# Two attention and long-convolution layers on one core: the scheduler's durations for fp32r matmuls, 32-column products and dots changed, and six more 512-wide buffers

## The chip, the cores and the metric

The kernel runs as one program on one core of a Trainium2 chip. The metric is the device time of one execution in microseconds; the time of a kernel is the median over several executions. The engines are TensorE (PE in the profile, with its weight loads as PEld), VectorE (DVE), ScalarE (ACT), GpSimd (POOL) and SyncE (SP), which issues all DMAs of this kernel.

## The reference

Two layers work on 256 latent tokens (x) and 256 context tokens (ctx), 2048 wide, in fp32. Cut to what matters:

```python
def _layer(x, ctx, c, c_ctx, lp, cos, sin, update_ctx):
    sh_x, sc_x, g_x = _modulation(c, lp["ada_w"], lp["ada_b"])       # silu(c) @ ada_w + ada_b, split in 3
    sh_c, sc_c, g_c = _modulation(c_ctx, lp["ada_w"], lp["ada_b"])
    hx = rmsnorm(x, lp["pre_g"]) * (1.0 + sc_x) + sh_x
    hc = rmsnorm(ctx, lp["pre_g"]) * (1.0 + sc_c) + sh_c
    px = hx @ lp["w_in"]                                             # 2048 x 5952
    pc = hc @ lp["w_in"]                                             # in the last layer only the k/v columns
    ...                                                              # latent attention, 8 heads, on q/kv columns
    ...                                                              # Hyena: width-3 conv, implicit filters, FFT conv
    y = concatenate([rmsnorm(o_mla) * silu(p_gm), rmsnorm(y_h) * silu(p_gh)])
    x_new = x + g_x * rmsnorm(y @ lp["w_out"], lp["post_g"])         # ctx likewise, in the first layer
```

`_modulation` is a matrix product of two vectors (c and c_ctx) with a 2048 x 6144 matrix in each layer: little arithmetic, 50 MB of weights a layer.

## The kernel before

**Arithmetic.** Each fp32 product is made of three fp32r matmuls: a weight and a token tile are each split into a rounded part (hi, a cast on ACT) and the rest (lo, a subtraction on DVE), and `mm3` multiplies hi by hi, hi by lo and lo by hi. In the first layer context and latent tokens are one 512-wide moving operand; in the second, and in the first layer's output projection, it is 256 wide.

**The order is made by a scheduler in the kernel's own Python.** `Net.run` holds a clock for each engine, written by durations that the helpers give (`mm`, `act`, `tt`, `dot`, `dma`). Jobs are generators that yield one operation at a time. At each step the scheduler takes, of the operations that can start within `WINDOW` of the first, the one whose job has the lowest rank, emits it, and moves the clock. The instruction order on every engine thus hangs on those durations; on the chip each engine runs its queue in that order and waits on semaphores. The durations set no time on the chip.

**The main line of work** is a fixed list of items, one each for a 128x1024 tile of weights, handled by three jobs: `loader` (DMA into a buffer), `prepper` (the split) and `products` (the matmuls into the PSUM tiles `acc`). Beside it run the side jobs on PSUM tiles `mis`: filters (`filt`), attention (`pair_job`, `qk_job`, `head_job`), Hyena (`hy_job`), norms, and the boundary between the layers. Products have the last rank, so they fill PE where no side step is ready.

**Buffers.** SBUF holds five 1024-wide `raw` and two `hi` tiles, and 82 tiles `s` of 128x512 (`N_SLOTS`) that all jobs share. The loader takes a `raw` tile where one is free (one DMA of 512 KB), and otherwise two `s` tiles (two DMAs of 256 KB) if at least `SPARE_RAW` = 12 are spare; the prepper does likewise with `SPARE` = 8.

**The start.** The products of the first layer need the modulated input, and so the modulation weights. They come in two ways. Most blocks go through PE: `ada_first` (weights `in_p_ada_first`, 128x128 against the 32-column tile `cs`, "32-column products"). The rest go through DVE: `ada_slow` (weights `in_p_ada_slow`) loads a weight tile into a ring of three buffers (`N_RING`) and makes dot products with a row of c or c_ctx that is spread over the partitions (`s<-crow_d`), by `dot`, one or two for each tile. The next tile for a ring buffer can be loaded when the dots on the old one are done, and SP's queue is in order: what is queued behind that load waits too. The first wave that runs, 16 ring loads and 32 dots, makes the first layer's shift for the last four of the 16 blocks of model columns; it takes four rounds, each with its own two `crow_d` loads. The sections in `ada_rest` are 32-column products with 512 wide weights, spread over the first layer.

Lines of the profile: L232 is `mm`, L235 a transpose, L243 and L245 `act`, L250 the DVE helpers, L280 `dot`, L309 `dma`.

Of the kernel before, what the change touches and what calls it, by code (L numbers as in the profile page):

```python
# [19 lines left out]
KT = 16  # L20
# [10 lines left out]

N_RAW = 5
N_HI = 2
N_SLOTS = 96 - 2 * (N_RAW + N_HI)
RESERVE = 1
SPARE = 8
SPARE_RAW = 12
# [45 lines left out]
def free_size(ap):  # L83
    n = 1
    for s in ap.shape[1:]:
        n *= s
    return n
# [82 lines left out]
class Net:  # L170
    def __init__(self, tc, pools, a):
# [6 lines left out]
        self.owner = None  # L178
        self.slots = Slots(self, sb, "s", N_SLOTS, [P, 512])
        self.raws = Slots(self, sb, "raw", N_RAW, [P, 1024])  # L180
# [44 lines left out]
    def mm(self, out, lhsT, rhs, start=True, stop=True, share=1.0):  # L225
        n = free_size(rhs)
        if lhsT.dtype == F32R:
            c = max(n, 480 if n < 256 else 0) / 2400 + 0.0025
        else:
            c = 4 * (n / 2400 + 0.0025) * share if n > 1 else 0.11  # L230
        return Op("pe", c, [out], [lhsT, rhs],
                  lambda: self.nc.tensor.matmul(out, lhsT, rhs, start=start, stop=stop), 0.2)  # L232

# [42 lines left out]
        return op  # L276

    def dot(self, junk, a, b, acc):
        return Op("dve", 0.07 + free_size(a) * 0.00104, [junk, acc], [a, b],
                  lambda: self.nc.vector.scalar_tensor_tensor(out=junk, in0=a, scalar=1.0, in1=b, op0=ALU.mult,  # L280
                                                              op1=ALU.mult, accum_out=acc))

# [339 lines left out]
    def ada_rest(self, which, l, sec):  # L622
        hold = {}
        out = []
        for kt in range(KT):
            def load(raws, kt=kt):
                for h in range(2):
                    yield from self.load(raws[h], self.a["p_ada_rest"][which, kt, h])

            def pe(raws, kt=kt):  # L630
                if kt == 0:
                    (hold["ps"],) = yield from self.pget()
                ps = hold["ps"]
                for c in range(4):
                    yield self.mm(ps[32 * c:32 * c + 32, :], self.cs[:, kt, :],
                                  raws[c // 2][:, (c % 2) * 512:(c % 2) * 512 + 512],
                                  kt == 0, kt == KT - 1, share=0.27)

            def post(kt=kt):
                if kt == KT - 1:  # L640
                    self.job(f"ada{l}_{sec}", self.ada_cols(l, sec, hold["ps"], [(4 * b, 4 * b + 4) for b in range(4)]), want=1)
            out.append(Item(load, None, pe, post, nraw=2, halves=True))
        return out
# [1193 lines left out]
```

## Time and profile before

| | |
|---|---|
| median of 3 runs | 1464.53 us (1457.56 to 1468.52) |
| the profiled execution | 1457.93 us; its span 1456.2 us |
| PE, share of the span | 98% |
| PEld | 85% |
| DVE | 82% |
| ACT | 48% |
| DMA, mean rate | 226 GB/s |

The span runs from the first to the last instruction. PE's busy share is made of modelled ends: matmuls overlap in the pipeline, so a row with no idle time can still hold gaps of some tens of ns, and the pace is better read from how many matmuls stand in a stretch of the chain of waits.

### The profile page before, as it was taken

The numbers are of one execution on the slowest core, as the hardware profiler recorded it, in microseconds if no ns is written. First come the engines' busy times: TensorE is split into PE (matmuls) and PEld (weight loads), VectorE is DVE, ScalarE is ACT, GpSimd is POOL, SyncE is SP. The second block draws the span as 40 slices with busy tenths as digits, with TensorE's granted clock in tenths as the row PEclk, the third lists the DMA queues.
The fourth block names the chain that finished last, engine by engine and source line by source line (L and its number), as shares of the span: only waits on it lengthen the run. The fifth ranks groups of instructions, "written<-read, shape, count | busy, mean of one in ns | idle before, by whom it ended". The sixth has DMA issues, their size and how long they took to land.

```text
span 1456.2 us, 25519 instructions
## 1 busy us (share of the span) xinstructions
PE 1428.0 (98%) x9316; PEld 1240.0 (85%) x9316; DVE 1188.4 (82%) x2514; ACT 692.0 (48%) x1323; POOL 16.4 (1%) x20
## 2 busy tenths in 40 slices
PE   7899999999999999999999999999999999999997
PEld 5677787778788887777779999999999999999886
DVE  5578989897899888998888887888977888796554
ACT  5421354335354552344324444566655667655542
POOL 0000000000000000000000000000000000000000
PEclk9999999999999999999999999999999999999999
DMA  9998875568466776557968885467728334658541
GB/s 319 350 355 262 293 263 200 164 216 307 159 210 220 252 276 227 180 194 231 318 189 301 297 283 197 167 222 247 254 88 319 113 105 149 236 199 293 174 145 58
DMA packets 165870, 328.88 MB, mean 226 GB/s; under 512 B 18501, under 2 KB 41068, under 8 KB 165744
## 3 DMA queue, kind: packets, MB, share of 16 engines
q1 hardware_dynamic: 165744, 327.25, 65.8%
q8 instruction: 73, 1.20, 0.3%
q14 instruction: 53, 0.43, 0.1%
HBM read 301.99 MB, written 25.18 MB: 225 GB/s over the span
## 4 chain that ended last, share of the span: by engine, by line
PE 87%; DMA 8%; DVE 2%; issue 1%; SPq 1%; ACT 1%; DVEq 0%; POOLq 0%; POOL 0%; ACTq 0%
PE acc L232 68%; PE mis L232 17%; PE mis L235 3%; DMA s<-in_p_ada_first 2%; DMA raw<-in_p_ada_first 1%; DMA raw<-in_p_win 1%; DVE s L250 1%; DMA s<-in_p_win 1%; SPq L309 1%; DMA s<-in_ctx 1%; DMA s<-xt_d 1%; DVE junk L280 0%; DMA s<-in_p_uv 0%; DMA s<-crow_d 0%; DVE raw L250 0%
## 5 line engine op out<-in xcount | busy, mean ns | idle before, releaser
L232 PE MATMUL acc<-s,hi 128*128 128x256 f32 (+1 forms) x2304 | 563.0, 335 | 0.7 <-ACT hi L243 0.6
L232 PE MATMUL acc<-s,s 128*128 128x256 f32 (+1 forms) x2976 | 485.8, 318 | 0.0
L232 PEld LDWEIGHTS acc<-s,s 128*128 128x128 f32 x2976 | 425.8, 191 | 39.1 <-issue 2.7
L232 PEld LDWEIGHTS acc<-s,hi 128*128 128x128 f32 x2304 | 388.4, 190 | 53.0 <-issue 8.8
L250 DVE TENSOR_TENSOR s<-s,s 128x512 fp32r<-128x512 f32 (+5 forms) x575 | 342.2, 623 | 40.0 <-ACT s L245 19.3
L232 PE MATMUL acc<-s,raw 128*128 128x256 f32 (+1 forms) x1104 | 369.8, 335 | 0.1
L280 DVE SCALAR_TENSOR_TENSOR junk<-s,s 128x512 bf16<-128x512 f32 x352 | 241.5, 686 | 24.8 <-DMA s<-in_p_ada_slow 8.4
L232 PE MATMUL mis<-s,s 128*128 128x256 f32 (+1 forms) x1232 | 239.6, 337 | 0.9 <-ACT s L243 0.9
L232 PEld LDWEIGHTS acc<-s,raw 128*128 128x128 f32 x1104 | 210.0, 190 | 21.5 <-DVE raw L250 1.2
L232 PEld LDWEIGHTS mis<-s,s 128*128 128x128 f32 x1232 | 189.6, 189 | 30.0 <-ACT s L243 2.4
L243 ACT CAST s<-s 128x512 fp32r<-128x512 f32 (+3 forms) x324 | 180.6, 589 | 71.9 <-DVE s L250 28.5
L243 ACT CAST hi<-raw 128x1024 fp32r<-128x1024 f32 (+1 forms) x100 | 97.2, 972 | 123.4 <-PE acc L232 55.4
L250 DVE TENSOR_TENSOR raw<-raw,hi 128x1024 fp32r<-128x1024 f32 x88 | 107.3, 1220 | 20.7 <-ACT hi L243 19.9
L243 ACT CAST hi<-s 128x512 fp32r<-128x512 f32 x124 | 73.4, 618 | 96.6 <-PE acc L232 74.4
L250 DVE TENSOR_TENSOR raw<-s,hi 128x512 fp32r<-128x512 f32 x124 | 83.9, 687 | 36.8 <-ACT hi L243 35.9
L243 ACT COPY s<-mis 128x512 f32<-128x512 f32 (+3 forms) x101 | 48.5, 485 | 114.3 <-PE mis L232 88.2
L250 DVE TENSOR_TENSOR s<-mis,s 128x512 fp32r<-128x512 f32 (+2 forms) x128 | 84.5, 669 | 19.7 <-ACT s L243 14.5
L243 ACT CAST s<-mis 128x512 fp32r<-128x512 f32 (+1 forms) x100 | 56.6, 570 | 82.8 <-PE mis L235 43.6
L245 ACT ACTIVATE s<-acc 128x256 f32<-128x256 f32 (+1 forms) x80 | 36.2, 455 | 82.6 <-PE acc L232 67.2
L235 PE MATMUL mis<-ident,s 128*128 128x128 f32 (+1 forms) x369 | 65.9, 289 | 6.3 <-DVE s L267 1.7
L250 DVE TENSOR_TENSOR s<-raw,s 128x512 fp32r<-128x512 f32 x106 | 69.7, 683 | 0.5 <-ACT s L243 0.4
L235 PEld LDWEIGHTS mis<-ident,s 128*128 128x128 f32 (+1 forms) x369 | 49.1, 155 | 20.5 <-ACT s L243 3.0
(85 smaller groups left out, 888.0 us busy)
## 6 DMA issues: line engine op xcount, KB each, us to landing
s<-in_p_ada_slow SPq DMA_DIRECT2D x208, 256.0 KB, 3.3
raw<-in_p_win SPq DMA_DIRECT2D x99, 512.0 KB, 5.3
s<-in_p_win SPq DMA_DIRECT2D x178, 256.0 KB, 5.4
s<-in_p_wout SPq DMA_DIRECT2D x108, 256.0 KB, 5.3
raw<-in_p_wout SPq DMA_DIRECT2D x42, 512.0 KB, 3.6
s<-in_p_ada_first SPq DMA_DIRECT2D x62, 256.0 KB, 6.2
raw<-in_p_ada_first SPq DMA_DIRECT2D x25, 512.0 KB, 6.0
raw<-in_p_ada_rest SPq DMA_DIRECT2D x20, 512.0 KB, 5.1
```

The lines of the kernel that those rows point to most:

```text
L232: lambda: self.nc.tensor.matmul(out, lhsT, rhs, start=start, stop=stop), 0.2)
L235: return Op("pe", 0.11, [out], [in_], lambda: self.nc.tensor.transpose(out, in_, ident), 0.2)
L243: self.nc.scalar.copy(out, in_)
L245: self.nc.scalar.activation(out, in_, func, **kw)
L250: return Op("dve", fixed + n * rate, [out], ins, lambda: getattr(self.nc.vector, name)(out=out, **kw))
L280: lambda: self.nc.vector.scalar_tensor_tensor(out=junk, in0=a, scalar=1.0, in1=b, op0=ALU.mult, op1=ALU.mult, accum_out=acc))
L309: return Op("sp", n / 360e3, [dst], [src], lambda: self.nc.sync.dma_start(dst, src))
```

## The change

Five numbers and one option.

- The duration of an fp32r matmul goes from n/2400 + 0.0025 us to n/2400 + 0.0137 us: 0.2158 to 0.2270 for 512 columns, 0.1092 to 0.1204 for 256. For plain fp32 the constant in each of four passes goes from 0.0025 to 0.003.
- The share of that duration which a 32-column product of 512 wide weights takes (`ada_rest`) goes from 0.27 to 0.37.
- The fixed part of a dot goes from 0.07 to 0.185 us: 0.602 to 0.717 for 512 elements.
- `N_SLOTS` goes from 82 to 88. The SBUF for it comes from `dynamic_dma_scratch_size=1024`, which makes the area that is kept for DMAs written by software smaller.

```diff
-N_SLOTS = 96 - 2 * (N_RAW + N_HI)
+N_SLOTS = 102 - 2 * (N_RAW + N_HI)
...
         if lhsT.dtype == F32R:
-            c = max(n, 480 if n < 256 else 0) / 2400 + 0.0025
+            c = max(n, 480 if n < 256 else 0) / 2400 + 0.0137
         else:
-            c = 4 * (n / 2400 + 0.0025) * share if n > 1 else 0.11
+            c = 4 * (n / 2400 + 0.003) * share if n > 1 else 0.11
...
     def dot(self, junk, a, b, acc):
-        return Op("dve", 0.07 + free_size(a) * 0.00104, [junk, acc], [a, b],
+        return Op("dve", 0.185 + free_size(a) * 0.00104, [junk, acc], [a, b],
...
-                                  kt == 0, kt == KT - 1, share=0.27)
+                                  kt == 0, kt == KT - 1, share=0.37)
...
-    nc = bacc.Bacc("TRN2", target_bir_lowering=False, num_devices=1)
+    nc = bacc.Bacc("TRN2", target_bir_lowering=False, num_devices=1, dynamic_dma_scratch_size=1024)
```

The program computes the same with the same 8750 PE instructions. On the other engines 37 loads of a 1024-wide tile become two of 512, with their splits in two as well: 37 DMAs more, 27 more instructions on DVE and 21 on ACT. The order is the same for the first stretch (on PE for the first 124 rows) and other from there on, on every engine. Two places follow.

SP's queue in the first wave of dots. Before, from the second round's rows of c (`crow_d`) on; the ring buffers are s_178, s_179 and s_180:

```order
L309 DMA s_219_1540<-crow_d 128x512
L309 DMA raw_32_1547<-in_p_ada_first 128x1024
L309 DMA s_178_1232<-in_p_ada_slow 128x512
L309 DMA raw_34_1586<-in_p_wkr 128x256
L309 DMA s_179_1233<-in_p_ada_slow 128x512
L309 DMA s_180_1234<-in_p_ada_slow 128x512
L309 DMA s_178_1232<-in_p_ada_slow 128x512
L309 DMA s_224_1646<-in_p_ada_first 128x512
L309 DMA s_225_1647<-in_p_ada_first 128x512
```

The change, at the same round; the ring buffers are s_182, s_183 and s_184:

```order
L309 DMA s_220_1514<-crow_d 128x512
L309 DMA raw_28_1518<-in_p_ada_first 128x1024
L309 DMA s_182_1236<-in_p_ada_slow 128x512
L309 DMA raw_30_1535<-in_p_wkr 128x256
L309 DMA s_221_1550<-in_p_ada_first 128x512
L309 DMA s_222_1551<-in_p_ada_first 128x512
L309 DMA s_229_1568<-in_k_decay 128x512
L309 DMA s_183_1237<-in_p_ada_slow 128x512
L309 DMA raw_31_1600<-in_p_ada_first 128x1024
L309 DMA s_184_1238<-in_p_ada_slow 128x512
```

Three ring loads stood in a row ahead of the modulation weights; now weights stand between them. One round later the change queues two ring loads in a row just behind the third round's `crow_d`, with eight halves of modulation weights behind them:

```order
L309 DMA s_235_1655<-crow_d 128x512
L309 DMA s_183_1237<-in_p_ada_slow 128x512
L309 DMA s_236_1684<-in_p_ada_first 128x512
L309 DMA s_237_1685<-in_p_ada_first 128x512
L309 DMA s_184_1238<-in_p_ada_slow 128x512
L309 DMA s_182_1236<-in_p_ada_slow 128x512
L309 DMA s_240_1720<-in_p_ada_first 128x512
L309 DMA s_241_1721<-in_p_ada_first 128x512
```

The last of these weights is s_247. Before, four stores of the filter spectrum (`kd`) stood ahead of the last weights; with the change they stand behind.

DVE in the same place. Before, the second round's dots (`junk`) with other work between:

```order
L280 SCALAR_TENSOR_TENSOR junk,s_177_1231<-s_179_1233,s_218_1538 128x512
L250 TENSOR_TENSOR s_124_775<-s_124_775,acc_30_1545 128x512
L250 TENSOR_TENSOR s_125_777<-s_125_777,acc_31_1546 128x512
L280 SCALAR_TENSOR_TENSOR junk,s_177_1231<-s_179_1233,s_219_1540 128x512
L250 TENSOR_TENSOR s_217_1522<-s_220_1572,s_221_1573 128x512
L280 SCALAR_TENSOR_TENSOR junk,s_177_1231<-s_180_1234,s_218_1538 128x512
```

The change, from the second round's last dot on buffer s_183 to the third round's first dots:

```order
L280 SCALAR_TENSOR_TENSOR junk,s_181_1235<-s_183_1237,s_220_1514 128x512
L250 TENSOR_TENSOR s_138_832<-s_138_832,acc_32_1615 128x512
L250 TENSOR_TENSOR s_139_834<-s_139_834,acc_33_1616 128x512
L280 SCALAR_TENSOR_TENSOR junk,s_181_1235<-s_184_1238,s_234_1653 128x512
L250 TENSOR_TENSOR s_232_1621<-s_232_1621,s_233_1622 128x512
L280 SCALAR_TENSOR_TENSOR junk,s_181_1235<-s_184_1238,s_235_1655 128x512
L250 TENSOR_TENSOR raw_32_1602<-s_217_1459,hi_7_1601 128x512
L280 SCALAR_TENSOR_TENSOR junk,s_181_1235<-s_182_1236,s_234_1653 128x512
```

The third round's dots, which need the rows s_234 and s_235, stand two additions behind the second round's last dot, and a split for the products (`raw_32`) stands behind two of them. Before, four other operations stood between those rounds.

## The prediction

> **What bounds the kernel now.** I read the page first, then the busy times by stage. The page's head:
>
> ```profile
> span 1456.2 us, 25519 instructions
> PE 1428.0 (98%) x9316; PEld 1240.0 (85%) x9316; DVE 1188.4 (82%) x2514; ACT 692.0 (48%) x1323; POOL 16.4 (1%) x20
> ```
>
> PE is busy for all but 28.2 us. The windows view says where those lie. Its columns are the stretch, its length, the busy time and instruction count of PE, PEld, DVE, ACT and POOL, then the granted PE clock, the DMA share and GB/s.
>
> ```profile
> 0.00:44.00 44.00, 32.70 (x336) 24.99 (x336) 19.93 (x54) 21.36 (x56) 1.32 (x6) 0.96 0.95 331
> 44.00:148.80 104.80, 102.58 (x853) 75.62 (x853) 79.85 (x168) 31.09 (x59) 0.00 (x0) 1.00 0.92 320
> 148.80:166.00 17.20, 15.05 (x170) 11.87 (x170) 16.84 (x38) 10.27 (x19) 0.00 (x0) 0.90 0.96 355
> 166.00:760.00 594.00, 592.29 (x2847) 472.79 (x2846) 529.11 (x1155) 253.14 (x441) 5.28 (x4) 1.00 0.67 225
> 760.00:1120.00 360.00, 359.09 (x2898) 352.95 (x2897) 303.22 (x642) 195.53 (x387) 6.85 (x6) 1.00 0.70 239
> 1120.00:1320.00 200.00, 199.08 (x1501) 189.99 (x1501) 168.18 (x337) 122.62 (x246) 1.81 (x2) 1.00 0.50 166
> 1320.00:1447.20 127.20, 127.15 (x720) 111.82 (x718) 67.61 (x118) 57.33 (x119) 0.55 (x1) 1.00 0.45 157
> 1447.20:1456.20 9.00, 0.00 (x0) 0.00 (x0) 3.65 (x7) 0.68 (x2) 0.55 (x1) 0.78 0.50 174
> ```
>
> PE idles 11.3 us (44.00 - 32.70) in the first stretch, 2.2 up to 148.8, 2.15 up to 166, then 1.7, 0.9, 0.9 and 0.05 in the four long stretches, and 9.0 after its last matmul. So from 166 us on PE sets the pace, and in over 1270 us it waits hardly at all. The waits view for PE from 166 to 1440 us is only this (who waited on whom: us in total, times, longest):
>
> ```profile
> PE mis L235 <- ACT s L245: 1.1, 1, 1.1
> PE mis L232 <- ACT s L243: 0.9, 1, 0.9
> PE mis L235 <- POOL rs L302: 0.7, 1, 0.7
> PE mis L235 <- DVE s L250: 0.4, 1, 0.4
> ```
>
> Four waits, 3.1 us. A scheduler with better durations can win them and little else there. The pace while PE runs, from the chain of waits (start, us, what):
>
> ```profile
> 697.58 18.41 PE acc L232 x81
> ...
> 1031.27 65.17 PE acc L232 x543
> ```
>
> 18.41/81 is 0.2273 us for a 512-wide matmul and 65.17/543 is 0.1200 for a 256-wide one. The change gives the scheduler 0.2270 and 0.1204, so its new numbers are this trace's. The chip's pace is not touched by them: PE has the same instructions afterwards, and what can move is only when it waits.
>
> **The change part by part.**
>
> *The first 148 us.* DMA sets the pace there. The one weak place is where SP stands behind the dots. By windows of 6 us:
>
> ```profile
> 114.00:120.00 6.00, 6.00 (x37) 3.94 (x36) 5.97 (x13) 2.39 (x4) 0.00 (x0) 1.00 0.78 242
> 120.00:126.00 6.00, 6.00 (x40) 4.62 (x40) 4.61 (x8) 0.88 (x2) 0.00 (x0) 1.00 0.95 251
> 126.00:132.00 6.00, 6.00 (x29) 4.23 (x23) 6.00 (x14) 0.41 (x1) 0.00 (x0) 1.00 0.48 151
> 132.00:138.00 6.00, 6.00 (x40) 4.55 (x40) 5.07 (x12) 0.00 (x0) 0.00 (x0) 1.00 0.59 188
> ...
> 150.00:156.00 6.00, 3.85 (x94) 2.59 (x87) 5.92 (x17) 3.50 (x9) 0.00 (x0) 0.93 1.05 394
> ```
>
> Against the 394 GB/s of the last row, the four before it move 152, 143, 243 and 206 GB/s less, 744 x 6 us = 4.5 MB, which is 11 us of DMA time. SP's timeline and its waits from 105 to 150 us tell why:
>
> ```profile
> 118.39 1.55 SPq L309 DMA_DIRECT2D s<-crow_d  x2
> ...
> 122.29 0.48 SPq L309 DMA_DIRECT2D raw<-in_p_wkr  x1
> 127.50 5.71 SPq L309 DMA_DIRECT2D s<-in_p_ada_slow  x3
> 133.26 3.08 SPq L309 DMA_DIRECT2D s<-in_p_ada_first  x6
> ...
> 147.74 0.33 SPq L309 DMA_DIRECT2D s<-in_p_ada_first  x1
> ```
>
> ```profile
> SPq L309 <- DVE junk L280: 13.0, 5, 4.6
> ```
>
> From 122.8 to 127.5 us nothing is issued. Then three ring loads go out, each when its buffer's dots are done, and six halves of modulation weights queue behind them until 133.3. The last half goes out at 147.7. PE needs it:
>
> ```profile
> 152.58 0.43 PE L232 MATMUL mis<-s,cs 128*32 128x128 f32 x8 [0.28 <-DMA s<-in_p_ada_first]
> 153.89 0.43 PE L232 MATMUL mis<-s,cs 128*32 128x128 f32 x8 [0.88 <-DMA s<-in_p_ada_first]
> ```
>
> This stall costs its idle time, 2.15 us, and a slow clock after it: 17.20 us at 0.90 granted is 1.7 us of PE time. Together 3.9 us is all that a perfect order wins here. PE's work ahead of this place is the same in both orders (the same items, and filter steps).
>
> The new SP order takes the three ring loads apart. Between the second round's `crow_d` and the first ring load that hangs on them stand a whole 512 KB tile, two halves, a decay tile and the k-rope tile, 1.4 MB beside a ring load, 4 us at 360 GB/s; before it was 0.65 MB. The four `kd` stores, 1 MB or 2.7 us, move behind the last weights. Against that, two ring loads now stand just behind the third round's `crow_d`, and eight halves wait for them. A `crow_d` load lands 5.7 us after its issue, then two dots on each buffer, at 0.69 us and as much for the operation between them, have to run: about 5.7 + 4 x 1.3 = 11 us from that `crow_d` to the eight halves, with 0.8 MB to move meanwhile. The last half would then land some 2 or 3 us earlier than the present 153.9. The rows:
>
> ```profile
> s<-crow_d SPq DMA_DIRECT2D x24, 256.0 KB, 5.7
> ```
>
> ```profile
> L280 DVE SCALAR_TENSOR_TENSOR junk<-s,s x352: 617/685/695, 105.0 to 895.6; 128x512 bf16<-128x512 f32 x176
> ```
>
> PE arrives at 148.8 and has about 4 us of 32-column products there (148.8 to 152.6), so weights that are 2 or 3 us earlier take away most of the idle time and with it the slow clock. I take 3 us of the 3.9; the bounds are a gain of 3.9 and, if the second block holds SP for as long as the first did beyond its cover, a loss of 5.7 (the 5.71 us of the three ring loads).
>
> *The dots.* The second number of that row is the median, 0.685 us, between the old 0.602 and the new 0.717. The dots keep their low rank; 352 x 0.115 = 40 us more of DVE time in the plan delays them against the products. Yet in the new order the last one stands behind less PE work than before, by about 160 256-wide matmuls or 19 us at the pace above. They end at 895.6 us, the boundary between the layers begins on them, and PE idles only 0.9 us in that stretch as it is; so the cover holds and grows, and this costs nothing. Without it PE would wait at the second layer's first products.
>
> *Six more buffers and 37 DMAs more.* Halves and whole tiles land alike:
>
> ```profile
> raw<-in_p_win SPq DMA_DIRECT2D x99, 512.0 KB, 5.3
> s<-in_p_win SPq DMA_DIRECT2D x178, 256.0 KB, 5.4
> ```
>
> A half more costs SP one issue: 3.08 us for six is 0.5, so 37 of them 19 us of a queue that has the whole span; four of the 37 fall into the modulation weights, 2 us at the most, on SP's free time there. From 166 us on DMA is at 0.50 to 0.70 of its time. The further instructions on DVE and ACT (27 and 21) lie beside PE. The smaller DMA area is used by none of these loads, which SP issues; I take nothing.
>
> *From 166 us on.* The order changes on all engines. The waits can go (-3.5 us: the idle 1.7 + 0.9 + 0.9) or others can come. A duration of PE that was 5% short was also a reserve: PE came later to every side step than planned. I take zero, with -3.5 and the second rival's +22 as ends.
>
> A page speaks against the new matmul numbers. The Trainium skill, "TensorE: Matmul & The Clock Gate", section "Back-to-back issue gap", gives N/2.4 + 2.5 ns for an isolated warm matmul, 215.8 ns at 512 columns: the old table. By it the 81 matmuls above would take 17.5 us; the trace has 18.41, so here the trace decides for the new number, and the sum is the same by both, since PE's time is the chip's and not the table's.
>
> *The sum.* The profiled execution took 1457.93 us, of which 1456.2 are the span. Less 3 us it is 1455. The median of the runs lies 6.6 us above that execution; from the median, 1464.5 - 3 gives 1461.5, and I say **1461 us**.
>
> **The rivals.** What can be told from no change I put at 1%, 14.6 us.
>
> *Nothing moves.* The second block of ring loads holds the last weights as long as the first did. For it: the four operations that stood on DVE between the rounds are now two, so a dot and what is queued behind it waits for the `crow_d`. Time 1464 to 1466. Chance 0.21.
>
> *All waits in the middle go.* 2.2 + 3.9 + 3.5 = 9.6 us from 44 us on, so 1455. Against it: only 3.1 us of waits are long enough to be named, and part of the 2.2 falls where the orders of DMA are still the same. Chance 0.12. The 11.3 and the 9.0 us at the ends stay in every case: the first rows are the same in both orders, and the end is the last norm.
>
> *Slower: side steps come to PE too early.* With true durations the scheduler places a side step on PE just when it expects its operand; a late ACT or DVE now holds PE's queue with all products behind it. In the profile before, ACT waits for PE at this step, and the one long case of the other kind costs 0.92 us:
>
> ```profile
> ACT s L243 <- PE mis L232: 90.4, 71, 3.1
> ```
>
> ```profile
> 1180.15 2.07 PE L232 MATMUL mis<-s,s 128*128 128x256 f32 x12 [0.92 <-ACT s L243]
> ```
>
> If of the 71 steps one in three turns round at that price, it is 24 x 0.92 = 22 us: 1486. From 16 steps on it is slower by over 1%. Against it: ACT is idle for half of the span and stands ready 1.3 us (90.4/71) before PE at these steps. Chance 0.15.
>
> **How the numbers follow.** The forecast has 0.52, these three 0.21, 0.12 and 0.15. Runs of one kernel spread over 1457.56 to 1468.52, about 5 us to each side. Faster by over 1% means under 1449.9: a fifth of the second rival (0.03), and 0.08 of the forecast and the first for spread and for gaps too short for the rows to name. Slower by over 1%, over 1479.2: most of the third rival (0.13) and 0.02 of the others. The rest, 0.74, is within 1%. The range runs from 1447, the second rival less its spread and some, to 1478, which takes in the 5.7 us of the early bound with its spread and half of the way into the third rival's waits; it leaves out about 2 in 10.
>
> **What would show it.** Right: no gap of 4 us in SP's issue behind the second `crow_d`; the last `in_p_ada_first` landing before 152 us; no idle row of PE and a clock near 1.00 between 148 and 166; PE's waits from 166 us on still some 3 us in all. Wrong: PE waits on ACT or DVE that sum to over 10 us after 166 us, DMA rows under 200 GB/s again between 125 and 145 us, or a PE pace other than 0.227 and 0.120.

## The result and the profile after

| | before | after |
|---|---|---|
| median | 1463.67 us (1457.56 to 1468.52, 4 runs) | 1479.84 us (1478.23 to 1483.18, 4 runs) |
| ratio to before, 95% interval | | 1.0105 [1.0083, 1.0127] |
| the profiled execution; its span | 1457.93 us; 1456.2 us | 1483.18 us; 1481.4 us |

The change makes the kernel 1% slower. The forecast of 1461 us was wrong: the time lies 1.8 us above its range, on the side of the rival in which side steps come to PE too early.

The busy times of the kernel after, by the same stages as before (columns: stretch, length, busy time and instructions of PE, PEld, DVE, ACT and POOL, granted PE clock, DMA share, GB/s):

```profile
0.00:44.00 44.00, 33.39 (x306) 25.36 (x308) 19.91 (x54) 20.93 (x54) 1.32 (x6) 0.96 0.95 327
44.00:148.80 104.80, 102.60 (x858) 75.82 (x855) 79.38 (x168) 29.95 (x57) 0.00 (x0) 0.98 0.93 319
148.80:166.00 17.20, 11.65 (x168) 8.64 (x167) 12.35 (x32) 7.37 (x15) 0.00 (x0) 0.80 0.99 365
166.00:760.00 594.00, 586.69 (x2801) 464.39 (x2800) 521.44 (x1145) 253.98 (x460) 4.81 (x4) 1.00 0.67 221
760.00:1120.00 360.00, 359.74 (x2832) 350.33 (x2831) 298.39 (x651) 185.68 (x373) 5.97 (x6) 1.00 0.68 230
1120.00:1320.00 200.00, 193.88 (x1428) 182.07 (x1427) 167.27 (x340) 120.44 (x246) 0.70 (x1) 1.00 0.49 165
1320.00:1447.20 127.20, 127.20 (x823) 116.61 (x822) 74.07 (x129) 62.31 (x124) 1.08 (x1) 1.00 0.59 200
```

PE idled 1.7 and 0.9 us in the stretches from 166 to 760 and from 1120 to 1320 us; now it is 7.3 and 6.1. The waits of PE from 166 to 1440 us (who on whom: us in total, times, longest), four before and 3.1 us in all, are now 17 and 13.0 us:

```profile
PE mis L232 <- ACT s L243: 5.7, 4, 2.7
PE mis L235 <- DMA s<-u_d: 2.5, 5, 0.7
PE mis L235 <- ACT s L245: 1.3, 2, 1.0
PE mis L235 <- DVE s L267: 1.1, 1, 1.1
PE mis L232 <- ACT s L245: 1.0, 1, 1.0
PE acc L232 <- DVE s L250: 0.7, 1, 0.7
PE mis L232 <- DVE s L250: 0.4, 2, 0.2
PE mis L235 <- DVE s L250: 0.3, 1, 0.3
```

All but one are first instructions of a side step (`mis`) whose operand was late. In PE's timeline from 1120 to 1320 us (start, us, what; in brackets the idle time before it and who ended it) one was named before (0.92 us on ACT, at 1180.15); now, in part:

```profile
1132.44 0.39 PE L232 MATMUL mis<-s,s 128*128 128x256 f32 x1 [0.74 <-ACT s L243]
...
1152.49 2.79 PE L232 MATMUL mis<-s,s 128*128 128x512 f32 x11 [1.03 <-ACT s L245]
...
1182.04 4.23 PE L232 MATMUL mis<-s,s 128*128 128x512 f32 x23 [1.26 <-ACT s L243]
...
1239.01 4.52 PE L232 MATMUL mis<-s,s 128*128 128x512 f32 x23 [1.07 <-ACT s L243]
```

The pace of PE's undisturbed runs has not changed. From the chain of waits (start, us, what), before and then after:

```profile
716.98 21.99 PE acc L232 x96
```

```profile
711.25 21.99 PE acc L232 x96
...
1031.04 71.06 PE acc L232 x589
```

A run of 96 512-wide matmuls takes the same 21.99 us, and 71.06/589 is 0.1206 us for a 256-wide one, beside 0.1200 before.

**A measure for the rest of the text.** Busy shares hide short gaps: a 512-wide matmul is shown with 0.39 us, though in an undisturbed run the next one starts 0.227 us after it. So I use a second measure. Every PE instruction is given the start-to-start interval that it has in an undisturbed run of the traces (0.2270 us for 512 columns, 0.120 for 256, 0.11 for transposes, and so on). The sum is 1383.5 us for every kernel here, since all have the same PE instructions. "Loss" is the time of the trace less this work: PE's idle time, its small gaps and its slow clock together. It can be read at any point of the work, so two orders can be compared at the same point. The table gives the loss of each kernel's profiled execution, one each, in four parts: the first 170 us of work (up to about 215 us of the span), the work from 170 to 850 us, the boundary between the layers (850 to 950), and the rest with the tail.

| kernel | median us | ratio, 95% interval | loss: first 170 | 170 to 850 | boundary | rest |
|---|---|---|---|---|---|---|
| before | 1463.67 to 1465.92 | | 44.1 | 13.5 | 1.5 | 13.5 |
| after | 1479.84 | 1.0105 [1.0083, 1.0127] | 51.3 | 23.8 | 1.2 | 21.6 |
| e1: matmul duration alone | 1503.73 | 1.0260 [1.0243, 1.0277] | 59.3 | 31.5 | 4.7 | 20.9 |
| e2: buffers alone | 1461.78 | 0.9981 [0.9966, 0.9996] | 42.8 | 10.3 | 8.6 | 18.2 |
| e3: dot duration alone | 1505.01 | 1.0264 [1.0244, 1.0284] | 49.1 | 14.7 | 42.1 | 15.9 |
| e4: all but the matmul duration | 1496.50 | 1.0213 [1.0196, 1.0230] | 44.0 | 13.2 | 40.0 | 12.9 |
| e5: all, with a longer lag | 1470.78 | 1.0052 [1.0033, 1.0070] | 50.1 | 17.7 | 0.6 | 14.5 |
| e6: dot duration, dots earlier | 1522.35 | 1.0408 [1.0386, 1.0430] | 49.7 | 71.6 | 0.9 | 14.4 |
| e7: constant 0.0030 | 1473.26 | 1.0071 [1.0048, 1.0093] | 54.5 | 17.5 | 0.9 | 12.5 |
| e8: constant 0.0081 | 1484.78 | 1.0145 [1.0112, 1.0177] | 58.2 | 23.7 | 1.9 | 14.6 |
| e9: new durations before 170 us | 1459.74 | 0.9964 [0.9948, 0.9980] | 45.5 | 11.3 | 1.1 | 13.0 |
| e10: new durations after 170 us | 1476.95 | 1.0079 [1.0055, 1.0102] | 43.9 | 27.0 | 2.1 | 19.8 |
| e11: e10, lag after ACT and DVE | 1467.85 | 1.0014 [1.0001, 1.0027] | 41.0 | 22.2 | 0.5 | 14.3 |
| e12: buffers, dots earlier | 1457.45 | 0.9952 [0.9936, 0.9968] | 44.5 | 13.3 | 0.7 | 14.2 |
| e13: e11, lag after all but PE | 1458.27 | 0.9955 [0.9939, 0.9971] | 42.6 | 18.2 | 0.7 | 12.2 |
| e14: e12, longer lag | 1455.04 | 0.9939 [0.9920, 0.9958] | 44.8 | 15.2 | 0.5 | 12.6 |
| e15: e12, still shorter matmuls | 1455.17 | 0.9937 [0.9916, 0.9959] | 40.7 | 8.9 | 4.2 | 16.3 |

After lost 25.3 us more than before in these two executions: 7.2 in the first part, 10.3 and 8.1 behind it, and nothing at the boundary. The medians are 16.2 us apart, 9 less: the profiled execution of before lies 6 us under its median, that of after 3 us over it. Where those 9 us lie is a finding of its own, below.

### The profile page after: what moved, and what is told of

Same layout as the page of the kernel before. It is cut to its first block, busy times and chain, and to the rows that moved or that the text cites. A ratio compares the mean times of both kernels' runs of the same rounds, so it can differ in the third digit from the quotient of the medians.

```text
span 1481.4 us, 25633 instructions
## 1 busy us (share of the span) xinstructions
PE 1440.8 (97%) x9316; PEld 1244.1 (84%) x9316; DVE 1187.7 (80%) x2541; ACT 688.8 (46%) x1344; POOL 15.0 (1%) x20
## 4 chain that ended last, share of the span: by engine, by line
PE 72%; DMA 13%; DVE 9%; issue 2%; SPq 2%; ACT 1%; DVEq 0%; POOLq 0%; POOL 0%; ACTq 0%
PE acc L232 57%; PE mis L232 13%; DVE s L250 6%; DMA s<-in_p_win 3%; PE mis L235 2%; SPq L309 2%; DMA s<-crow_d 2%; DMA s<-in_p_ada_slow 1%; DMA s<-in_p_uv 1%; DVE junk L280 1%; DMA s<-u_d 1%; DMA s<-in_p_ada_first 1%; DMA s<-in_ctx 1%; ACT s L243 1%; DMA s<-kd 1%
## 5 line engine op out<-in xcount | busy, mean ns | idle before, releaser
L232 PE MATMUL acc<-s,s 128*128 128x256 f32 (+1 forms) x3420 | 560.4, 319 | 0.0
L232 PEld LDWEIGHTS acc<-s,s 128*128 128x128 f32 x3420 | 489.8, 191 | 46.7 <-issue 2.8
L232 PE MATMUL acc<-s,hi 128*128 128x256 f32 (+1 forms) x2000 | 490.8, 336 | 5.9 <-ACT hi L243 5.1
L250 DVE TENSOR_TENSOR s<-s,s 128x512 fp32r<-128x512 f32 (+6 forms) x605 | 359.7, 626 | 40.2 <-ACT s L243 18.3
L232 PEld LDWEIGHTS acc<-s,hi 128*128 128x128 f32 x2000 | 338.9, 191 | 51.9 <-issue 8.0
L232 PE MATMUL acc<-s,raw 128*128 128x256 f32 (+1 forms) x952 | 319.9, 336 | 0.0
L243 ACT CAST s<-s 128x512 fp32r<-128x512 f32 (+3 forms) x354 | 195.9, 591 | 70.0 <-DVE s L250 27.4
L232 PEld LDWEIGHTS acc<-s,raw 128*128 128x128 f32 x952 | 181.3, 190 | 18.6 <-issue 0.9
L243 ACT CAST hi<-raw 128x1024 fp32r<-128x1024 f32 (+1 forms) x76 | 71.9, 947 | 136.0 <-PE acc L232 113.0
L250 DVE TENSOR_TENSOR raw<-raw,hi 128x1024 fp32r<-128x1024 f32 x64 | 78.1, 1220 | 40.4 <-ACT hi L243 39.9
L250 DVE TENSOR_TENSOR s<-mis,s 128x512 fp32r<-128x512 f32 (+2 forms) x128 | 84.6, 668 | 19.0 <-ACT s L243 17.7
```

What stands on the lines that cost most here:

```text
L243: self.nc.scalar.copy(out, in_)
L250: return Op("dve", fixed + n * rate, [out], ins, lambda: getattr(self.nc.vector, name)(out=out, **kw))
```

## The experiments

**The parts alone.** Four kernels split the change. The first takes only the duration of the fp32r matmul:

```diff
-            c = max(n, 480 if n < 256 else 0) / 2400 + 0.0025
+            c = max(n, 480 if n < 256 else 0) / 2400 + 0.0137
```

> Of the change, only the fp32r matmul's duration (0.0025 to 0.0137). Theory R (lost reserve: with true PE durations side steps stand on PE just when their operands are due, and any lateness holds PE): this part makes most of the loss, 1474 to 1480 us, and PE's waits on ACT and DVE after 166 us sum to over 8 us. Rival L (any new order of this program loses, whatever the number that was changed): also 1470 to 1480, so this run alone tells R from the rivals D and S, not from L. Rival D (the dots) and S (the buffers): within 1459 to 1468.

1503.73 us, ratio 1.0260, 24 us above what was expected. The loss is in no one place: 15 us more than before in the first part, 18 in the next, 3 at the boundary, 7 in the rest. PE's waits from 166 to 1440 us come to 26 us; the longest groups of them:

```profile
PE mis L232 <- DVE s L250: 5.4, 10, 2.8
PE mis L235 <- ACT s L245: 4.5, 4, 2.6
PE mis L232 <- ACT s L243: 4.0, 4, 2.0
```

The second takes only the buffers (`N_SLOTS` 88 and the smaller DMA area):

> Of the change, only the six buffers with the smaller DMA area; all durations as before. Theory R: within 1459 to 1468, since PE's reserve is untouched. Rival S (more prefetch in halves collides or delays the queue): 1472 or more. Rival L: 1470 to 1480.

1461.78 us, ratio 0.9981 [0.9966, 0.9996]. The buffers cost nothing, as expected. In the profiles they gain 4.5 us up to 850 us of work and lose 11.8 from there on, 7.1 of it where the second layer begins, and the last dot starts later than before's (911.4 and 895.6 us).

The third takes only the dot, the fourth takes everything but the matmul:

```diff
-        return Op("dve", 0.07 + free_size(a) * 0.00104, [junk, acc], [a, b],
+        return Op("dve", 0.185 + free_size(a) * 0.00104, [junk, acc], [a, b],
```

> Of the change, only the dot's duration (fixed part 0.07 to 0.185). Theory R: within 1459 to 1468. Rival D (the dots' new places hold SP's ring loads and the first products): 1468 to 1475, lost before 170 us. Rival L: 1470 to 1480.

> The whole change without the fp32r matmul's new duration (0.0025 again). Theory R: most of the loss goes, 1460 to 1468, and the waits of PE after 166 us are near 3 us again. Rivals D and S: the loss stays, 1475 to 1483. Rival L: 1470 to 1480 with waits of PE like the change's.

1505.01 and 1496.50 us. Both miss: the theory had them within 1459 to 1468, and the rival that blames the dots looked for the loss before 170 us. Both lose it in one stall of about 40 us at the boundary. Of the dots alone, the waits of PE from 166 us on, and the dots themselves ("to" stands between the starts of the first and of the last):

```profile
PE mis L232 <- DVE s L250: 30.1, 5, 24.8
```

```profile
L280 DVE SCALAR_TENSOR_TENSOR junk<-s,s x352: 615/685/694, 106.3 to 959.3; 128x512 bf16<-128x512 f32 x176
```

The last dot starts at 959.3 us and not at 895.6. Everywhere else these two kernels lose about what before does (the dots alone 5 us more in the first part). So the two durations are coupled. A longer dot pushes the dots, which have the lowest rank but one, behind the first layer's last products. A longer matmul gives the plan more time beside each product, and the dots come back. In the whole change the last one starts at 893.9 us and the boundary costs 1.2 us.

**The reserve.** The theory after these four was that the matmul duration, 5% short, had been a reserve: with the true number a side step is put on PE when its operand is just due. If so, the loss goes when the reserve is put back in another place. The plan has one: `lag`, the time from an operation's end to its reader's start, 0.15 us for all but PE, which has 0.2. The fifth kernel is the whole change with

```diff
-    def __init__(self, eng, cost, outs, ins, emit, lag=0.15, other=None):
+    def __init__(self, eng, cost, outs, ins, emit, lag=0.45, other=None):
...
-WAVE0 = (((1, 2, 0, 16), (1, 1, 0, 16)), ("hx0_12",), 9.5)
-WAVE1 = (((1, 0, 0, 16),), ("slow0",), 9.5)
+WAVE0 = (((1, 2, 0, 16), (1, 1, 0, 16)), ("hx0_12",), 8.5)
+WAVE1 = (((1, 0, 0, 16),), ("slow0",), 8.5)
```

> The whole change, with the reserve put back where it belongs and not in the matmul's duration: the time from an operation's end to its reader's start is planned as 0.45 us and not 0.15 for every ACT and DVE operation, and the two waves of dots get rank 8.5 and not 9.5, so that the longer lag doesn't push the last dot behind the boundary. Theory 'lost reserve' (true matmul durations make the scheduler place side steps on PE just when the operand is due, and PE waits whenever it is late): the waits of PE from 166 us on fall from 13 us to under 6, their idle time there from 18 us to under 7, and the time is 1458 to 1468, ratio 0.995 to 1.003. Rival 'any new order loses, since the old one was picked for what it does': 1473 to 1488, with 12 us or more of waits. Theory 'the buffers or the halves cost it': 1475 to 1485, since they are still in.

This edit raises a default that loads have as well as ACT and DVE, so it is wider than its expectation says. 1470.78 us: that misses the expected time by 3 us but gives back 9 of the 16. Behind the first part the loss falls from 46.6 us to 32.8 (before 28.5), and PE's waits from 166 us on from 13.0 us to 7.2, not under 6; the first part keeps its 50.

**The boundary.** The sixth kernel has the longer dots alone, with the rank of the two late waves at 6.5 so that they can't be pushed behind the boundary:

> Only the dot's new duration, as in the run that gave 1505 us, with the rank of the two waves of dots 6.5 instead of 9.5, which brings their last dot forward to well before the last product of the first layer. Theory 'longer dots are planned late and the boundary waits for them': the stall of about 40 us at the layer boundary is gone, the last dot ends before 880 us, and the time is 1460 to 1472. Rival 'the new order alone costs it': the dot's order still loses 25 us or more, 1490 or above.

1522.35 us, a miss. The boundary's stall is gone as expected (0.9 us instead of 42), but a larger one stands some 250 us earlier. PE's timeline there:

```profile
721.87 0.60 PE L235 MATMUL mis<-ident,s 128*128 128x128 f32 x4
750.45 0.80 PE L232 MATMUL mis<-s,s 128*128 128x512 f32 x1 [27.98 <-ACT s L243]
...
768.41 1.01 PE L232 MATMUL mis<-ones,s 128*128 128x1 f32 x4 [6.96 <-DVE s L250]
```

ACT waited up to 14.2 us for DVE meanwhile, and DVE was busy for 26.9 us of the 28, 14.2 of them with dots. With rank 6.5 the dots pass the side steps on which PE waits. So the place of the dots costs about 40 us on the late side and 58 on the early one. Rank 8.5, which six other kernels here have, loses at most 0.7 us at the boundary in five of them and 4.2 in the sixth.

**Is it the reserve, or is any new order worse?** The seventh kernel is the one before with 0.0030 in place of 0.0025: another order on every engine, nothing truer. The eighth has 0.0081, half of the way.

```diff
-            c = max(n, 480 if n < 256 else 0) / 2400 + 0.0025
+            c = max(n, 480 if n < 256 else 0) / 2400 + 0.0030
```

> The kernel before with the constant of the fp32r matmul 0.0030 and not 0.0025, a fifth of a percent of a matmul: nothing in the plan is truer or falser for it, but the order is another one on every engine from the first hundred rows on. Theory 'lost reserve': the reserve is the same, so 1458 to 1469, ratio 0.995 to 1.003, waits of PE from 166 us on under 6 us. Rival 'any new order loses': 1472 to 1485, with the waits of 10 us or more spread over the span.

> The kernel before with the constant of the fp32r matmul 0.0081, half of the way to 0.0137, nothing else changed. The full way alone gave 1503.7 us. Theory 'lost reserve': the loss grows as the reserve shrinks, so between the two, 1470 to 1495, with PE's waits from 166 us on between 8 and 22 us. Rival 'any new order loses': no dose, 1472 to 1504 wherever it falls, not told apart by this alone. If it is at 1465 or below, the loss comes only close to the true duration, where the reserve is almost gone.

1473.26 and 1484.78 us. By its time the first of the two goes to the rival: a new order alone cost 9 us. But not in the manner that the rival named. PE's waits from 166 us on are 3.7 us, as before's, and its stages there show no loss either; it is all in the first part:

```profile
44.00:148.80 104.80, 100.72 (x837) 74.04 (x832) 80.10 (x169) 30.20 (x58) 0.00 (x0) 0.98 0.90 305
148.80:166.00 17.20, 11.50 (x160) 6.15 (x158) 14.41 (x38) 6.12 (x12) 0.00 (x0) 0.77 1.02 379
```

Before moved 320 GB/s in the first of these stretches, this kernel 305, and PE then idled 5.7 us at a slow clock. The eighth kernel lies where it was expected, with 8.6 us of waits. So there are two things, and the table keeps them apart. The first part, which DMA feeds through a queue that stands behind the dots, is 10 to 15 us worse in these profiles, most of it at the first small step of the constant: 54.5, 58.2 and 59.3 us of loss at 0.0030, 0.0081 and 0.0137, beside before's 44.1. Some 5 us of such a difference can belong to the execution (last section), so its size is less sure than that of the medians. With the six buffers it is 41 to 51 us; whether they are what protects it was not isolated. Behind it (170 to 850, and the rest) the loss follows the constant: 27.0 us at 0.0025, 30.0 at 0.0030, 38.3 at 0.0081, 52.4 at 0.0137.

**Early and late apart.** In the ninth kernel the new durations hold only while the scheduler's clock is below 170 us, in the tenth only from there on; both have the buffers.

```diff
-            c = max(n, 480 if n < 256 else 0) / 2400 + 0.0137
+            c = max(n, 480 if n < 256 else 0) / 2400 + (0.0137 if self.now < 170.0 else 0.0025)
```

> The whole change, but the new durations hold only while the scheduler's clock stands below 170 us; from there on the old ones. The six buffers stay. So the order up to about 150 us of PE's queue is the changed kernel's, and the rest is planned with the old reserve. Theory 'two losses that add up' (about 8 us before 170 us, from the order of ring loads, dots and weights, and about 10 us after it, from the lost reserve): the early loss is kept and the late one goes, so 1468 to 1474, with PE's idle time up to 166 us as in the changed kernel (about 20 us) and its waits from 166 us on under 7 us. If the loss is all of the late kind: 1462 or below. If it is all early: 1478 to 1484.

> The mirror image: the old durations while the scheduler's clock stands below 170 us, the new ones from there on, with the six buffers. The order up to 166 us is then that of the kernel with the buffers alone. Theory 'two losses that add up': the early loss goes, the late one stays, 1469 to 1475, with PE's waits from 166 us on at 10 us or more and its idle time up to 166 us at most 17 us. If the loss is all early: 1462 or below.

1459.74 and 1476.95 us. The first is below what was expected and 0.36% faster than before; the second is 2 us above its range and nearly as slow as the whole change. So the loss is of the late kind, and I had put too much of it in the first part. PE's waits of the tenth kernel from 166 us on, where before had 3.1 us, begin with

```profile
PE mis L235 <- DMA s<-u_d: 6.5, 5, 3.4
PE mis L232 <- DVE s L250: 4.2, 8, 1.7
PE mis L235 <- ACT s L245: 3.7, 3, 2.7
```

**The reserve again, without the early order.** The eleventh kernel is the tenth with a lag longer by 0.30 us behind ACT and DVE from 170 us on, and the late dots at rank 8.5. The thirteenth has that lag behind loads and POOL too.

```diff
-            self.wrote[k] = max(self.wrote.get(k, 0.0), end + op.lag)
+            self.wrote[k] = max(self.wrote.get(k, 0.0), end + op.lag + (0.3 if op.eng in ('act', 'dve') and t > 170.0 else 0.0))
```

> As the one before (new durations only from 170 us on), with the reserve put back beside them: from 170 us on every ACT and DVE operation is planned to reach its reader 0.30 us later (0.45 and not 0.15), and the two late waves of dots have rank 8.5 and not 9.5. Theory 'lost reserve': the late loss goes as well, 1457 to 1464, ratio 0.993 to 1.000, and the waits of PE from 166 us on are under 6 us. Rival 'any new order loses': 1469 or above, as without the lag.

> As the run with the new durations and the 0.30 us of lag from 170 us on (1467.9 us), but with the lag behind DMA loads and POOL operations too. There the waits that stayed were on u_d loads (3.0 us) and on POOL (2.5 us). Theory 'what is left are the operands without a lag': these two waits fall under 2 us together and the time to 1458 to 1464. If the rest has another cause (order by chance): 1466 to 1472 again.

1476.95 us becomes 1467.85 with the lag on two engines, short of what was expected (the waits fall from 16.9 us to 11.0, not under 6), and 1458.27 with it on all but PE: 18.7 us below the same durations without the lag, and below before (ratio 0.9955 [0.9939, 0.9971]). The rank, which changed with the lag, was not run alone here; the boundary, for which it was changed, is 1.4 us of the difference in the profiles. The weight loads of side steps from 166 to 1440 us show it best (groups of instructions; the last column is PEld's idle time just before them, with who ended it). Before, after, and the thirteenth kernel:

```profile
L232 PEld LDWEIGHTS mis<-s,s 128*128 128x128 f32 x1216 | 186.8, 189 | 28.7 <-ACT s L243 2.3 <-DVE s L250 2.2 <-ACT hi L243 0.8
```

```profile
L232 PEld LDWEIGHTS mis<-s,s 128*128 128x128 f32 x1216 | 186.5, 190 | 41.3 <-ACT s L243 10.0 <-DVE s L250 5.0 <-issue 1.6
```

```profile
L232 PEld LDWEIGHTS mis<-s,s 128*128 128x128 f32 x1216 | 185.8, 190 | 27.3 <-issue 1.9 <-ACT s L243 1.5 <-DVE s L250 1.4
```

What `s` tiles from ACT and DVE ended of it goes from 4.5 us to 15.0 and back to 2.9 with the same true matmul duration in the plan. What was expected of the single waits was not met: those on `u_d` loads and POOL fell from 5.5 us to 4.1, not under 2. So the time was right, but which operands the last 9.6 us came from isn't shown. The fifth kernel, whose longer lag takes in loads but not POOL, lies between the two behind the first part (37.0, 32.8 and 31.1 us of loss), which speaks for the loads; these are single executions of different orders.

**More reserve.** The twelfth kernel is the one with the buffers alone and the late dots at rank 8.5. The fourteenth adds 0.15 us of lag behind ACT and DVE from 170 us on; the fifteenth takes 0.0065 off the matmul constant instead (to -0.0040), also from 170 us on.

> The version meant to beat both: the six buffers alone, with every old duration, and the two late waves of dots at rank 8.5 instead of 9.5. With the buffers alone (1461.8 us, ratio 0.998) PE lost about 8 us where the second layer begins, because the last dots stood behind the first layer's last products. With the rank the order has the last dot about 11 us of PE's work ahead of the last of these products. Theory 'the boundary waits for the dots': these 8 us go, 1452 to 1458, ratio 0.991 to 0.996. If the dots only shift the stall to their own place, as rank 6.5 did with the longer dots: 1460 or above.

> The six buffers, old durations, the late dots at rank 8.5 (1457.5 us), and from 170 us on a lag of 0.30 and not 0.15 us behind every ACT and DVE operation: more reserve than the kernel before had. If the old reserve was too small: 1450 to 1455. If it was enough: 1455 to 1461, since PE's idle time between 166 and 1440 us is only some 4 us there. If every new order loses: 1463 or above.

> The same kernel with the six buffers and rank 8.5, with no longer lag, but from 170 us on the fp32r constant is -0.0040 and not 0.0025: a matmul 3% shorter still in the plan, so that the reserve grows by half of what the change took from it (0.0065 beside 0.0112). The last dot moves to about 7 us of PE's work behind the last product before the boundary's first load, which may cost up to 8 us there. Lost reserve: outside of the boundary PE loses no more than with the old duration; 1455 to 1466 in all. If a wrong duration is bad in either direction (the optimum lies near the truth or at the old value by chance): 1468 or above, with waits of PE spread from 166 us on.

1457.45, 1455.04 and 1455.17 us, all faster than before. The first and the third lie where they were expected; the second stands on the line between "too small" and "enough". In the twelfth the last dot starts 49 us earlier than with the buffers alone (911.4 us there), and the boundary costs 0.7 us instead of 8.6:

```profile
L280 DVE SCALAR_TENSOR_TENSOR junk<-s,s x352: 670/685/695, 104.7 to 862.6; 128x512 bf16<-128x512 f32 x176
```

The two with more reserve gain 2 us more, which their intervals don't tell apart from the twelfth. So more of it doesn't hurt, and a wrong duration isn't bad in itself: at -0.0040 the plan is further from the trace than before's was, and the loss behind the first part, without the boundary, is 25.2 us, the second least of the table. Before had about enough. The two fastest kernels of the study are these two, 0.6% faster than before.

**Order by chance?** The table answers it for the work behind the first part, the boundary left out ("170 to 850" and "rest" together). Nine kernels plan there with the old duration, 0.0030 or a shorter one, in nine orders, and lose 24 to 31 us (the sixth, with its stall of dots, is left out). The three with the true duration and the old lag lose 45 to 52, the one half of the way 38, and the three with the true duration and a longer lag 30 to 37. So an order by itself moves this loss by up to 7 us, and the step beyond that goes with the reserve.

## Why the prediction was wrong, point by point

**What bounds the kernel: right.** PE sets the pace from 166 us on, its pace is the same, and what moved was waits, short gaps and the clock behind them.

**The first 148 us: half right, with no gain to be seen.** The step said that the new order takes the first block of ring loads apart, that the second block doesn't hold SP long, and that the last modulation weights come 2 or 3 us earlier. SP's timeline of after (start, us, what):

```profile
123.10 0.58 SPq L309 DMA_DIRECT2D s<-in_k_decay  x1
126.37 0.33 SPq L309 DMA_DIRECT2D s<-in_p_ada_slow  x1
...
132.19 1.12 SPq L309 DMA_DIRECT2D s<-crow_d  x2
...
134.63 0.89 SPq L309 DMA_DIRECT2D s<-in_p_ada_first  x2
139.80 2.75 SPq L309 DMA_DIRECT2D s<-in_p_ada_slow  x2
142.60 3.93 SPq L309 DMA_DIRECT2D s<-in_p_ada_first  x8
...
148.11 1.65 SPq L309 DMA_DIRECT2D kd<-s  x3
150.17 1.03 SPq L309 DMA_DIRECT2D s<-crow_d  x2
...
152.83 1.22 SPq L309 DMA_DIRECT2D raw<-in_p_win  x2
```

The first gap is 2.7 us instead of 4.7, and from the third round's `crow_d` to the eight halves it is 10.4 us (132.19 to 142.60), close to the step's 11. But there the second block holds SP for 4.3 us (135.52 to 139.80), as the rival "nothing moves" had it, and DMA falls under 200 GB/s again, which the prediction had named as a sign of being wrong:

```profile
138.00:144.00 6.00, 5.93 (x37) 3.87 (x35) 5.47 (x14) 0.00 (x0) 0.00 (x0) 1.00 0.52 167
```

The last weights go out by 146.5 us, 1.5 us earlier than before, and PE no longer waits for them. What is late next was not asked. Before, the first load of `w_in` stood right behind the last weights:

```profile
148.41 0.33 SPq L309 DMA_DIRECT2D s<-in_p_win  x1
```

With the change four stores, two rows of c and two ring loads stand ahead of it, it goes out at 152.83 us, and PE waits for that one:

```profile
154.76 1.49 PE L232 MATMUL mis<-s,cs 128*32 128x128 f32 x48
...
162.08 1.22 PE L232 MATMUL acc<-s,hi 128*128 128x512 f32 x2 [5.12 <-ACT hi L243]
```

So a wait of 2 us moved down the queue and became one of 5. The kernel with this same early order and the old durations behind it takes 1459.74 us, so this isn't what made the change slow; but no row shows the 3 us of gain either.

**The dots: right in the sum, by luck of the pair.** "Costs nothing" holds in the whole change (1.2 us at the boundary). The cover that the step names was there, and its price without it, which the prediction only named, is 40 us. That the cover hung on the matmul duration of the same change wasn't seen.

**Buffers and 37 DMAs: right.** The kernel with the buffers alone issues 39 DMAs more than before, and its ratio is 0.9981.

**From 166 us on: this step failed.** It took zero between -3.5 and +22. In the profiles it is 18.4 us of loss (10.3 + 8.1), and in medians the new durations there alone cost 12 us beside before, 15 beside the buffers alone, and 20 where the early order is the changed one (1479.84 beside 1459.74). The step named the mechanism, "a duration of PE that was 5% short was also a reserve", and the third rival priced it: from 16 turned steps on slower by over 1%, at 0.92 us each. Measured are 17 waits of 0.8 us, 13.0 us, 10.5 of them on ACT and DVE (the prediction's sign of being wrong was 10), and more gaps too short for that view. What stood against the rival was wrong: ACT waits for PE at 71 steps and stands ready 1.3 us ahead on the mean. After, the same row reads

```profile
ACT s L243 <- PE mis L232: 78.4, 63, 3.0
```

1.2 us ahead on the mean, at 63 steps, in a kernel that is 1% slower. The row is of ACT waiting for what PE writes; whether PE finds its own operand ready is the other direction, which the row doesn't measure. And the lead of the steps at which ACT is early says nothing of those at which it is late, and those are the ones that count. 0.15 was too little for the only rival that a duration change acts on directly, at every side step of PE.

## What to carry to other kernels

In a planned order like this one the durations aren't only estimates: what they fall short of the truth on the bounding engine is slack for every operand that engine waits for. Correct such a number only together with the lag that is planned at each hand-off, for all producers (engines and loads), and ask of every low-rank job what it is planned behind when another number moves. And before reading a difference of two profiles as the change's, see in which stage the two executions of one order can differ.

## What the runs showed that was not expected

**Two executions of the same queues, over 5 us apart after 160 us.** After and the ninth kernel have the same order on all engines up to about 180 us. Yet the first product behind the wait for `w_in`, at 162.08 us in after's row above, stands in the ninth kernel's timeline at

```profile
156.75 1.22 PE L232 MATMUL acc<-s,hi 128*128 128x512 f32 x2 [4.27 <-ACT hi L243]
```

and the stretch ahead of it, beside after's row of the windows, reads

```profile
44.00:148.80 104.80, 103.50 (x883) 76.30 (x885) 82.37 (x176) 30.73 (x60) 0.00 (x0) 1.00 0.96 337
```

337 GB/s against 319, with the same loads in the same order. The wait for `w_in` itself is in both (5.1 and 4.3 us) and so belongs to the order. But some 5 us in the part of the kernel that DMA feeds belong to the execution and not to the order; the 11 us over which before's first four runs spread leave room for that. The record doesn't say on which chip after ran, so a difference between chips isn't excluded; before's medians on the three chips of the experiments lie within 1464 to 1466 us. Of the 7.2 us by which the profiles of before and after differ in the first part, most can be this, though a reading of these two profiles alone would put all of it down to the change.

**An idle PE costs its clock behind it.** In windows of 6 us, after:

```profile
156.00:162.00 6.00, 0.58 (x13) 0.14 (x1) 4.27 (x13) 1.28 (x3) 0.00 (x0) 0.73 1.00 385
162.00:168.00 6.00, 5.88 (x18) 4.29 (x19) 5.94 (x15) 4.66 (x10) 0.00 (x0) 0.70 0.95 344
168.00:174.00 6.00, 6.00 (x28) 4.97 (x27) 6.00 (x15) 2.09 (x3) 0.00 (x0) 1.00 0.65 214
```

A wait of 5.1 us is followed by 6 us at 0.70, which is 1.8 us more. The Trainium skill, "TensorE: Matmul & The Clock Gate", section "What's actually happening", has half clock after an idle window of about 3.4 us and full clock after a busy one; 3.4 us at half clock would be 1.7 us by it, an estimate that this row agrees with.
